# Seven-product SwiGLU in a hybrid decoder trunk: sums and casts behind the evictions, modulation blocks in a load order of their own

## The chip, the core and the metric

One NeuronCore of a Trainium2 chip runs the whole program. The metric is device time in microseconds (us) from launch to end; lower is better. TensorE does the matmuls, VectorE (DVE), ScalarE (ACT) and GpSimd (POOL) the elementwise work, and SyncE (SP) issues nearly all loads. Each engine works its own instructions strictly in the order in which the program wrote them, and waits for the others by semaphores.

## The reference, cut to what matters

Two layers, each: a SwiGLU half step, a mixer (retention, two convolutions), a second SwiGLU half step. Input: 512 prompt tokens and 64 sample tokens, 576 columns in all, model width 1024, inner width 2816, everything in float32.

```python
ada = silu(c) @ w_ada + b_ada            # 9 modulation vectors per sequence and layer
h = rms_norm(x, g) * (1 + scale) + shift
x = x + 0.5 * gate * ((silu(h @ w1) * (h @ w3)) @ w2)
...                                      # mixer, then the same SwiGLU with other weights
```

## The kernel before, in words

**Precision.** A float32 product is made from three matmuls of halves: every operand is split into `hi` (a rounded copy, made by ScalarE) and `lo` (the difference, made by VectorE), and `hi*hi + hi*lo + lo*hi` is summed in PSUM (lines 267 to 269 and 533 to 535). The weights are split in the kernel: `raw` tiles arrive by DMA in four buffers (`RAW`), ScalarE casts `hi` (lines 180 and 194), VectorE subtracts `lo` (line 129, called by `rest`), and five pairs of `hi` and `lo` buffers (`WB`, counted by `live`) hold the results.

**Tiling.** The 576 columns are worked in two halves of 288 (`HB`). One matmul is 128 x 128 weights against 128 x 288 columns. The inner width is 22 blocks `f` of 128 columns of w1 and of w3.

**Seven products.** For f = 4 to 21 two neighbouring blocks of one weight are taken together (a "duo") and the 2 x 2 block product is made with seven block products instead of eight, as Strassen and Winograd do. `duo_step(f, up)` does it for w1 (up = 0) and then for w3 (up = 1) by calling `seven`. In `seven` the seven products run one after another on TensorE, 12 matmuls each, into four PSUM banks: X0 into p, Y0 into q, X1 on top of p, Z0 on top of q, S into r, Y1 into t, Z1 on top of r. ScalarE copies p away between X0 and X1 (line 542, called s1 here), because X1 goes on accumulating on p; VectorE adds s1 and q (line 546, called u here) between Y0 and Z0. Each finished quarter goes to `post`: for up = 0 the silu (`up1`), for up = 1 the product with the silu and the split into `ghi` and `glo` (`up3`; line 835 on POOL, 838 on ACT, 839 on DVE). The sums of weight blocks that the scheme needs are made by POOL: `sums` (lines 204 and 205) when a pair of raw tiles is taken up, and `z` (lines 209 and 210) as a job of its own. The jobs of the next pair (cast X, sums z, casts S, Y, Z) are emitted one by one by `pump`.

**Differences of h.** The scheme also needs sums and differences of h's blocks: `forms` makes them, four rounds of POOL adds (`za`, `zb`, lines 491 and 492), four VectorE operations (495 to 498), ScalarE casts (501 and 502) and VectorE subtractions (504 and 505), a step at a time while the first pairs f = 0 to 3 run as plain products. `last_forms` (lines 517 and 518) then overwrites the second half of four rows of `hh` and `hl` in place, once f = 3 is through.

**Order.** The program is written out by hand: a list of steps (`steps`) is walked once, and `pump` is called at many points. It issues DMAs on SP in the order of one list of keys (raw weights and modulation blocks mixed, in the order of use), emits casts, and emits jobs. In the first SwiGLU of layer 0 and in the second one the modulation matmuls (`ada_unit`, line 332) are sown in between the steps: two units after each duo step and, in the second, after each down step too (one there in the first). After eight units `ada_unit` copies PSUM to SBUF on VectorE (line 337), and `ada_done` transposes the copy on TensorE (line 348) at the next opportunity: at the start of a duo step, of a down step, or in `tick`. `down` does the product with w2: for each of the four groups of f (`GROUPS`) eight down steps, one per block of 128 output columns; a post of them is three VectorE operations (728, 731, 734) and one on POOL.

Below are the functions that the diff touches and what calls them.

Of the kernel before, what the change touches and what calls it, by code (L numbers as in the profile page):

```python
# [69 lines left out]
class Trunk:  # L70
    def __init__(self, nc, tc, d, o, ctx):
# [14 lines left out]
        self.later = []  # L86
        self.quota = 0
# [30 lines left out]
    def start(self):  # L118
# [5 lines left out]
        self.n_dma = self.held = self.whole = self.live = self.cur = 0  # L124
# [6 lines left out]
    def pump(self, later=False):  # L131
        nc = self.nc
        once = False
        while True:
            went = False
            if self.n_dma < len(self.keys) and self.keys[self.n_dma][0] == "do":
# [3 lines left out]
            elif self.n_dma < len(self.keys) and self.keys[self.n_dma][0] == "ada":  # L140
                if self.whole < (ADA if self.quota < 9 else ADA_LATER) and self.n_dma <= self.cur + 2 * ADA:
                    key = self.keys[self.n_dma]
                    self.split[key] = self.slot([128, 512], what="ada")
                    nc.sync.dma_start(self.split[key], self.source(key)[0])
                    self.n_dma += 1
                    self.whole += 1
                    went = True
# [8 lines left out]
            if self.jobs:  # L156
                if not (later and once) and self.live + self.jobs[0][0] <= WB:
# [4 lines left out]
            elif self.raw and self.quota and self.order[self.raw[0][0]] <= self.order[self.cur] + AHEAD:  # L162
# [70 lines left out]
    def free(self, key):  # L233
        if key[0] == "ada":
            self.whole -= 1
# [247 lines left out]
    def forms(self):  # L483
# [4 lines left out]
        zs = []  # L488
        for i in range(4):
            za, zb = self.slot([128, NT], what="za"), self.slot([128, NT], what="zb")  # L490
            nc.gpsimd.tensor_add(za, self.hh[:, i, :NT].bitcast(F32), self.hl[:, i].bitcast(F32))
            nc.gpsimd.tensor_add(zb, self.hh[:, i + 4, :NT].bitcast(F32), self.hl[:, i + 4].bitcast(F32))
            yield
# [15 lines left out]
            zs.append(za)  # L509
# [11 lines left out]
    def seven(self, key, post):  # L521
# [16 lines left out]
        free = lambda which: self.free((*key, which))  # L538
        p, q = bank(), bank()
# [3 lines left out]
        self.rest()  # L543
# [3 lines left out]
        self.rest()  # L547
# [3 lines left out]
        self.rest()  # L551
# [3 lines left out]
        self.rest()  # L555
# [4 lines left out]
        self.rest()  # L560
# [4 lines left out]
        self.rest()  # L565
# [3 lines left out]
        self.rest()  # L569

# [42 lines left out]
    def begin(self, l, sh, pairs, post, forms=()):  # L613
# [26 lines left out]
        for n, pair in enumerate(pairs):  # L640
            hooks = {k: more for k in (1, 3, 5)}
# [103 lines left out]
    def ffn(self, l, ab, sh, fill, first, last):  # L745
# [5 lines left out]
        def post(pair, half, ps):  # L751
            nc = self.nc
            f = pair[0][2]
            if half == 0:
# [28 lines left out]
        def pair_step(pair):  # L783
            ws = [self.use(k) for k in pair]
            for half in range(2):
                ps = []
                for w, k in zip(ws, pair):
                    ps.append(self.run(w, self.h, half))
                    if half == 1:
                        self.free(k)  # L790
                    self.tick()
                post(pair, half, ps)

# [847 lines left out]
```

## Time and profile before

| | |
|---|---|
| median of 3 runs | 3319.72 us (3313.78 to 3321.75) |
| profiled execution | 3321.77 us |
| its span, first to last instruction | 3320.0 us |
| mean granted TensorE clock | 0.964 of full |
| TensorE busy with matmuls | 3072.1 us, 93% of the span |
| VectorE, ScalarE, POOL busy | 1981.4, 1033.6, 1013.0 us |

The profile is of one execution; its own time is 2.05 us above the median. Waits are told as "instruction that waited <- instruction that released it". A matmul's duration in the profile overlaps the next one's, so TensorE's pace is read from counts in a stretch, not from durations. TensorE's clock has two levels here, 2.4 GHz (granted 1.00) and 1.2 GHz (granted 0.50).

### The profile page before, as it was taken

Reading aid. Unit: us, or ns where it says so; the run is one execution under the profiler, and the core shown is the slowest. Engines: PE = TensorE matmul, PEld = TensorE weight load, DVE = VectorE, ACT = ScalarE, POOL = GpSimd, SP = SyncE. Lnnn points to the kernel's source line nnn. Section 1 sums busy time; section 2 is a strip of 40 time slices with the busy share of each in tenths; the row PEclk is TensorE's granted clock in tenths of the full one; section 3 lists DMA queues with packets and bytes.
Section 4 is the critical chain, followed back from the end, with each engine's and each line's share of the span. In section 5 each row is a group of like instructions: output and inputs, shape, how many; then the busy total and the mean of one; then the engine's idle time right before and its main releaser. Section 6 shows DMA issues by size and latency. Waiting matters only on the chain. (4 is left out here: it accounts for less than half of the span.)

```text
span 3320.0 us, 55694 instructions
## 1 busy us (share of the span) xinstructions
PE 3072.1 (93%) x22548; PEld 2928.9 (88%) x22548; DVE 1981.4 (60%) x3545; ACT 1033.6 (31%) x1761; POOL 1013.0 (31%) x985
## 2 busy tenths in 40 slices
PE   7899989999999998798898999999999999989998
PEld 5788888899999997787797989888999999988997
DVE  6454566356995464444567556663569954666566
ACT  4232333222233332222233333332222333333332
POOL 3242344223122031323324334442231220324352
PEclk9999999999999999898998999999999999989999
DMA  6354423335322313534421222233352223122222
GB/s 236 114 177 164 149 74 115 116 90 118 88 77 89 96 61 131 178 131 168 147 90 48 80 89 77 79 119 114 90 118 88 77 89 96 64 65 78 78 87 67
DMA packets 147298, 349.70 MB, mean 105 GB/s; under 512 B 32912, under 2 KB 37264, under 8 KB 147040
## 3 DMA queue, kind: packets, MB, share of 16 engines
q1 hardware_dynamic: 140384, 329.35, 31.2%
q0 software_dynamic: 5504, 15.61, 1.8%
q8 instruction: 177, 2.90, 0.4%
q10 hardware_dynamic: 1152, 1.18, 0.1%
q14 instruction: 81, 0.66, 0.1%
HBM read 328.90 MB, written 12.45 MB: 103 GB/s over the span
## 5 line engine op out<-in xcount | busy, mean ns | idle before, releaser
L129 DVE TENSOR_TENSOR lo<-raw,hi 128x1024 fp32r<-128x1024 f32 (+2 forms) x553 | 704.0, 1278 | 424.1 <-ACT hi L180 330.4
L267 PE MATMUL pl<-hh,hi 128*128 128x288 f32 x2320 | 695.9, 300 | 23.6 <-ACT t L758 23.0
L268 PE MATMUL pl<-hl,hi 128*128 128x288 f32 x2320 | 689.5, 297 | 9.1 <-POOL hl L476 6.4
L269 PE MATMUL pl<-hh,lo 128*128 128x288 f32 x2320 | 688.4, 297 | 1.5 <-DVE lo L129 1.5
L180 ACT CAST hi<-raw 128x1024 fp32r<-128x1024 f32 (+2 forms) x337 | 315.9, 944 | 590.0 <-PE pl L268 316.1
L267 PEld LDWEIGHTS pl<-hh,hi 128*128 128x128 f32 x2320 | 440.2, 190 | 31.3 <-ACT t L758 23.9
L268 PEld LDWEIGHTS pl<-hl,hi 128*128 128x128 f32 x2320 | 440.1, 190 | 12.3 <-POOL hl L476 7.7
L533 PE MATMUL pl<-hh,hi 128*128 128x288 f32 x1152 | 363.2, 315 | 84.7 <-ACT t L542 65.3
L269 PEld LDWEIGHTS pl<-hh,lo 128*128 128x128 f32 x2320 | 439.7, 190 | 1.9 <-DVE lo L129 1.9
L267 PE MATMUL pl<-ghi,hi 128*128 128x288 f32 x1408 | 426.0, 303 | 5.8 <-ACT hi L180 5.8
L269 PE MATMUL pl<-ghi,lo 128*128 128x288 f32 x1408 | 420.7, 299 | 3.4 <-DVE lo L129 3.2
L268 PE MATMUL pl<-glo,hi 128*128 128x288 f32 x1408 | 420.2, 298 | 0.2
L534 PE MATMUL pl<-hl,hi 128*128 128x288 f32 x1152 | 357.5, 310 | 4.6 <-DVE hl L518 4.6
L535 PE MATMUL pl<-hh,lo 128*128 128x288 f32 x1152 | 357.5, 310 | 1.6 <-DVE lo L129 1.6
L533 PEld LDWEIGHTS pl<-hh,hi 128*128 128x128 f32 x1152 | 232.4, 202 | 98.3 <-ACT t L542 69.3
L267 PEld LDWEIGHTS pl<-ghi,hi 128*128 128x128 f32 x1408 | 269.4, 191 | 22.0 <-issue 12.3
L194 ACT CAST hi<-raw 128x1024 fp32r<-128x1024 f32 x216 | 224.4, 1041 | 158.8 <-PE pl L268 89.9
L269 PEld LDWEIGHTS pl<-ghi,lo 128*128 128x128 f32 x1408 | 268.9, 191 | 5.2 <-DVE lo L129 5.2
L268 PEld LDWEIGHTS pl<-glo,hi 128*128 128x128 f32 x1408 | 269.1, 191 | 1.1 <-DVE glo L839 1.1
L737 POOL TENSOR_TENSOR xs<-xs,t 128x64 f32<-128x64 f32 x144 | 65.4, 455 | 648.2 <-DVE t L734 644.8
L534 PEld LDWEIGHTS pl<-hl,hi 128*128 128x128 f32 x1152 | 233.4, 203 | 5.6 <-DVE hl L518 5.6
L535 PEld LDWEIGHTS pl<-hh,lo 128*128 128x128 f32 x1152 | 233.1, 202 | 2.1 <-DVE lo L129 2.1
(247 smaller groups left out, 6133.9 us busy)
## 6 DMA issues: line engine op xcount, KB each, us to landing
ada<-in_ada SPq DMA_DIRECT2D x288, 256.0 KB, 4.1
raw<-in_win SPq DMA_DIRECT2D x120, 512.0 KB, 3.6
raw<-in_w1a SPq DMA_DIRECT2D x44, 512.0 KB, 3.9
raw<-in_w3a SPq DMA_DIRECT2D x44, 512.0 KB, 4.3
raw<-in_w1b SPq DMA_DIRECT2D x44, 512.0 KB, 3.6
raw<-in_w3b SPq DMA_DIRECT2D x44, 512.0 KB, 4.2
raw<-in_w2a SPq DMA_DIRECT2D x48, 384.0 KB, 3.3
raw<-in_w2b SPq DMA_DIRECT2D x48, 384.0 KB, 3.5
```

The lines of the kernel that those rows point to most:

```text
L129: self.nc.vector.tensor_sub(lo, t, hi.bitcast(F32))
L180: nc.scalar.copy(hi[:, :m], t[:, c])
L194: self.nc.scalar.copy(w[0][:, :n], t[:, :n])
L267: mm(ps[:, :HB], hi[:, c], x[0][:, t], start=first, stop=False)
L268: mm(ps[:, :HB], hi[:, c], x[1][:, t], start=False, stop=False)
L269: mm(ps[:, :HB], lo[:, c], x[0][:, t], start=False, stop=last)
L533: mm(ps, hi[:, c], x[0], start=first and i == 0, stop=False, **k)
L534: mm(ps, hi[:, c], x[1], start=False, stop=False, **k)
L535: mm(ps, lo[:, c], x[0], start=False, stop=last and i == 3, **k)
L737: nc.gpsimd.tensor_add(xs, xs, t[:].rearrange("p b t -> p (b t)"))
```

## The change

- `seven`: `part` no longer calls `pump`. After each product's eviction a new `more()` runs the pending `lo` subtractions (`rest`), then whatever lies in `self.after`, then `pump(True)`; after the last product comes `pump(True, False)`, which emits no job but may take up the next pair (`sums`) or a plain cast. So casts and POOL sums now stand behind the eviction that they used to stand in front of. `ada_done` is called inside `seven`, after the third product, and no more at the start of a duo step or of a single down step.
- `up3`: the ScalarE cast of `ghi` is put off together with the subtraction of `glo`, to the next post; the last one of a seven goes into `self.after`, so behind the next seven's s1 (at the end of a group it is done at once).
- `pump`: at most one job per call, and no cast or `sums` after a job in the same call. Once the kernel is under way (`quota > 8`) modulation blocks are taken out of the common list into a queue of their own (`adas`), so raw weights are no longer held up behind them; a used modulation block counts as free only three calls of `pump` later (`gone`).
- `forms`: POOL makes `za` one round ahead, `zb` goes to VectorE, each round is two steps instead of three; `begin` takes two steps per pair (after k = 2 and 5) instead of three.
- f = 3 runs its second half first, and `last_forms` is emitted between the halves.

```diff
+        self.adas, self.gone = deque(), deque()
...
-    def pump(self, later=False):
+    def load_ada(self, key):
+        self.split[key] = self.slot([128, 512], what="ada")
+        self.nc.sync.dma_start(self.split[key], self.source(key)[0])
+        self.whole += 1
+
+    def pump(self, later=False, cast=True):
         nc = self.nc
-        once = False
+        once = not cast
+        self.calls += 1
+        while self.gone and self.gone[0] <= self.calls:
+            self.gone.popleft()
+            self.whole -= 1
         while True:
             went = False
+            if self.quota > 8:
+                while self.n_dma < len(self.keys) and self.keys[self.n_dma][0] == "ada":
+                    self.adas.append(self.n_dma)
+                    self.n_dma += 1
+                if self.adas and self.whole < ADA_LATER and self.adas[0] <= self.cur + 2 * ADA:
+                    self.load_ada(self.keys[self.adas.popleft()])
+                    went = True
...
-                if not (later and once) and self.live + self.jobs[0][0] <= WB:
+                if not once and self.live + self.jobs[0][0] <= WB:
...
-            elif self.raw and self.quota and self.order[self.raw[0][0]] <= self.order[self.cur] + AHEAD:
+            elif self.raw and self.quota and not (once and cast) and self.order[self.raw[0][0]] <= self.order[self.cur] + AHEAD:
...
     def part(self, key, which):
         self.cur = max(self.cur, self.at[key])
-        self.pump(True)
         return self.split[(*key, which)]
...
         if key[0] == "ada":
-            self.whole -= 1
+            if self.quota > 8:
+                self.gone.append(self.calls + 3)
+            else:
+                self.whole -= 1
...
+        whole_a(0)
+        yield
         for i in range(4):
-            za, zb = self.slot([128, NT], what="za"), self.slot([128, NT], what="zb")
-            nc.gpsimd.tensor_add(za, self.hh[:, i, :NT].bitcast(F32), self.hl[:, i].bitcast(F32))
-            nc.gpsimd.tensor_add(zb, self.hh[:, i + 4, :NT].bitcast(F32), self.hl[:, i + 4].bitcast(F32))
-            yield
+            if i < 3:
+                whole_a(i + 1)
+            za, zb = zs[i], self.slot([128, NT], what="zb")
+            nc.vector.tensor_add(zb, self.hh[:, i + 4, :NT].bitcast(F32), self.hl[:, i + 4].bitcast(F32))
...
+        def more():
+            self.rest()
+            for fn in self.after:
+                fn()
+            self.after = []
+            self.pump(True)
+
...
         nc.scalar.copy(s1, p)
-        self.rest()
+        more()
         product(q, "Y", 0, self.T[7], True, True)
...
         post(0, 0, p)
-        self.rest()
+        more()
+        self.ada_done()
...
         post(0, 1, u, r)
         self.rest()
+        self.pump(True, False)
...
-            hooks = {k: more for k in (1, 3, 5)}
+            hooks = {k: more for k in (2, 5)}
...
-            for half in range(2):
+            halves = (1, 0) if pair[0][2] == 3 else (0, 1)
+            for half in halves:
...
+                if half > halves[1]:
+                    self.drain()
+                    self.last_forms()
...
-            self.ada_done()
             if up == 0:
...
-                nc.scalar.copy(hi, s)
-                waiting.append(lambda: nc.vector.tensor_sub(lo, s, hi.bitcast(F32)))
+
+                def halves():
+                    nc.scalar.copy(hi, s)
+                    nc.vector.tensor_sub(lo, s, hi.bitcast(F32))
+
+                waiting.append(halves)
...
-            for fn in waiting:
-                fn()
+            self.after += waiting
+            if f + 2 in [at for at, _ in GROUPS] + [FT]:
+                for fn in self.after:
+                    fn()
+                self.after = []
...
-            self.ada_done()
+            if len(keys) > 1:
+                self.ada_done()
```

## Rows read from the trace of the kernel before

**Rows 1.** The first lines of the profile's page: the span, and busy us, share of the span and count of each engine.
```profile
span 3320.0 us, 55694 instructions
PE 3072.1 (93%) x22548; PEld 2928.9 (88%) x22548; DVE 1981.4 (60%) x3545; ACT 1033.6 (31%) x1761; POOL 1013.0 (31%) x985
```
**Rows 2.** Busy time by stretch: start and end, length, then busy us and count of each engine, granted clock, DMA share and GB/s. The first four are the four SwiGLU stages (the first and second of layer 0, then of layer 1), the last an undisturbed stretch of the mixer.
```profile
60.00:528.00 468.00, 422.21 (x3226) 392.52 (x3224) 258.91 (x421) 145.36 (x243) 157.05 (x134) 0.96 0.41 134
1217.00:1738.00 521.00, 449.76 (x3386) 415.90 (x3384) 263.38 (x435) 147.04 (x250) 160.29 (x138) 0.91 0.40 136
1769.00:2189.00 420.00, 387.06 (x2794) 384.54 (x2792) 260.61 (x409) 145.87 (x250) 161.51 (x138) 0.95 0.26 80
2876.00:3295.00 419.00, 385.58 (x2789) 383.06 (x2789) 258.47 (x406) 143.53 (x247) 161.27 (x138) 0.96 0.23 71
1079.00:1162.00 83.00, 83.00 (x629) 83.00 (x628) 38.72 (x66) 29.05 (x50) 2.79 (x6) 1.00 0.31 96
```
**Rows 3.** The same stretches, TensorE's matmuls into the `pl` banks alone (the 128 x 288 products).
```profile
60.00:528.00 468.00, 393.35 (x2764) 0.96 0.41 134
1217.00:1738.00 521.00, 411.34 (x2792) 0.91 0.40 136
1769.00:2189.00 420.00, 387.06 (x2794) 0.95 0.26 80
2876.00:3295.00 419.00, 385.58 (x2789) 0.96 0.23 71
```
**Rows 4.** Waits of TensorE over the whole run: who waited for whom, us in total, how often, the longest.
```profile
PE pl L533 <- ACT t L542: 65.3, 17, 5.8
PE pm L348 <- DVE t L337: 53.5, 17, 13.1
PE pl L267 <- ACT t L758: 23.0, 4, 8.1
...
PE pl L533 <- ACT hh L517: 14.6, 3, 7.0
...
PE pl L533 <- DVE t L546: 6.7, 5, 1.6
...
PE pl L267 <- ACT hi L180: 5.8, 7, 1.3
PE pl L269 <- DVE lo L129: 4.7, 9, 0.7
PE pl L534 <- DVE hl L518: 4.6, 4, 1.6
```
**Rows 5.** Waits of TensorE in the stage 1769 to 2189 alone, the first line.
```profile
PE pl L533 <- ACT t L542: 20.0, 5, 4.0
```
**Rows 6.** POOL in order of time, in two places of the stage 1769 to 2189: start us, us, instruction, idle time before it and what ended it.
```profile
1793.66 1.28 POOL L209 TENSOR_TENSOR raw<-raw,s 128x512 f32<-128x512 f32 x1 [11.88 <-issue]
...
1796.26 1.41 POOL L491 TENSOR_TENSOR za<-hh,hl 128x576 f32<-128x576 f32 x1
...
1904.43 0.96 POOL L835 TENSOR_TENSOR t<-t,t 128x288 f32<-128x288 f32 x1 [2.16 <-DVE t L834]
...
1906.98 2.28 POOL L204 TENSOR_TENSOR s<-raw 128x512 f32<-128x512 f32 x1
1909.33 1.38 POOL L205 TENSOR_TENSOR raw<-raw,raw 128x512 f32<-128x512 f32 x1
1910.67 1.77 POOL L835 TENSOR_TENSOR t<-t,t 128x288 f32<-128x288 f32 x1
```
**Rows 7.** ACT in order of time, in the same two places, and in a down step of the stage 1217 to 1738 (the first line).
```profile
1344.65 0.83 ACT L180 CAST hi<-raw 128x768 fp32r<-128x768 f32 x1 [10.79 <-DMA raw<-in_w2b]
...
1803.06 0.67 ACT L501 CAST thi<-zb 128x576 fp32r<-128x576 f32 x1 [10.79 <-DVE zb L498]
...
1912.48 0.43 ACT L838 CAST ghi<-t 128x288 fp32r<-128x288 f32 x1 [4.04 <-POOL t L835]
1912.82 1.04 ACT L194 CAST hi<-raw 128x1024 fp32r<-128x1024 f32 x1
1913.76 0.39 ACT L542 COPY t<-pl 128x288 f32<-128x288 f32 x1
```
**Rows 8.** DVE in order of time, in the same two places.
```profile
1797.70 1.63 DVE L495 TENSOR_TENSOR za<-za 128x288 f32<-128x288 f32 x1 [4.17 <-POOL za L491]
...
1903.05 0.68 DVE L129 TENSOR_TENSOR lo<-s,hi 128x512 fp32r<-128x512 f32 x1
...
1904.27 0.45 DVE L839 TENSOR_TENSOR glo<-t,ghi 128x288 fp32r<-128x288 f32 x1
...
1908.39 1.19 DVE L839 TENSOR_TENSOR glo<-t,ghi 128x288 fp32r<-128x288 f32 x1
1909.50 2.30 DVE L129 TENSOR_TENSOR lo<-raw,hi 128x1024 fp32r<-128x1024 f32 x1
...
1913.89 1.23 DVE L129 TENSOR_TENSOR lo<-raw,hi 128x1024 fp32r<-128x1024 f32 x1 [0.49 <-ACT hi L194]
```
**Rows 9.** TensorE's modulation matmuls of one down step of the stage 1217 to 1738, in order of time: two units.
```profile
1337.17 1.07 PE L332 MATMUL pm<-ada,cs 128*32 128x256 f32 x16
```
**Rows 10.** SP's four DMA issues right behind them.
```profile
1337.83 1.75 SPq L144 DMA_DIRECT2D ada<-in_ada  x4
```
**Rows 11.** The page's DMA issues: count, KB each, median us from issue to landing.
```profile
ada<-in_ada SPq DMA_DIRECT2D x288, 256.0 KB, 4.1
```

More of the change, by code (lines that the diff above doesn't have):

```diff
@@ L123, in start @@
         self.raw, self.late, self.split, self.jobs = deque(), deque(), {}, deque()
-        self.n_dma = self.held = self.whole = self.live = self.cur = 0
+        self.n_dma = self.held = self.whole = self.live = self.cur = self.calls = 0
+        self.adas, self.gone = deque(), deque()
     def rest(self):
@@ L140, in pump @@
             elif self.n_dma < len(self.keys) and self.keys[self.n_dma][0] == "ada":
[L141 to L144, printed above, removed]
+                if self.whole < ADA and self.n_dma <= self.cur + 2 * ADA:
+                    self.load_ada(self.keys[self.n_dma])
                     self.n_dma += 1
-                    self.whole += 1
                     went = True
@@ L487, in forms, with whole_a @@
         self.T = {2: [], 4: [], 5: []}
-        zs = []
+        zs = [None] * 4
+        def whole_a(i):
+            zs[i] = self.slot([128, NT], what="za")
+            nc.gpsimd.tensor_add(zs[i], self.hh[:, i, :NT].bitcast(F32), self.hl[:, i].bitcast(F32))
+        whole_a(0)
+        yield
         for i in range(4):
-            za, zb = self.slot([128, NT], what="za"), self.slot([128, NT], what="zb")
-            nc.gpsimd.tensor_add(za, self.hh[:, i, :NT].bitcast(F32), self.hl[:, i].bitcast(F32))
-            nc.gpsimd.tensor_add(zb, self.hh[:, i + 4, :NT].bitcast(F32), self.hl[:, i + 4].bitcast(F32))
-            yield
+            if i < 3:
+                whole_a(i + 1)
+            za, zb = zs[i], self.slot([128, NT], what="zb")
+            nc.vector.tensor_add(zb, self.hh[:, i + 4, :NT].bitcast(F32), self.hl[:, i + 4].bitcast(F32))
             a, b = slice(0, HB), slice(HB, NT)
@@ L508, in forms @@
             self.T[4].append((hi[:, a], lo[:, a]))
-            zs.append(za)
             yield
@@ L550, in seven @@
         post(0, 0, p)
-        self.rest()
+        more()
+        self.ada_done()
         product(q, "Z", 0, self.T[2], False, True)
@@ L554, in seven @@
         nc.vector.tensor_sub(u, u, q)
-        self.rest()
+        more()
         r = bank()
@@ L559, in seven @@
         post(1, 1, v, r)
-        self.rest()
+        more()
         t = bank()
@@ L564, in seven @@
         post(1, 0, v, t)
-        self.rest()
+        more()
         product(r, "Z", 1, quarter(1, 1), False, True)
@@ L753, in post @@
             f = pair[0][2]
-            if half == 0:
+            if f not in g:
                 g[f] = (self.slot([128, NT], F32R, "ghi"), self.slot([128, NT], F32R, "glo"))
@@ L788, in pair_step @@
                     ps.append(self.run(w, self.h, half))
-                    if half == 1:
+                    if half == halves[1]:
                         self.free(k)
@@ L799, in one_pair @@
             pair_step(pairs[f])
-            if f == 3:
-                self.drain()
-                self.last_forms()
         acts = {}
@@ L850, in duo_step @@
             self.seven(pairs[f][up], late if up else up1)
-            for fn in waiting:
-                fn()
+            self.after += waiting
+            if f + 2 in [at for at, _ in GROUPS] + [FT]:
+                for fn in self.after:
+                    fn()
+                self.after = []
             if up and f + 2 == FT:
```

## The prediction, made before the changed kernel was built or run

> **What bounds the kernel now.** I read the page first: TensorE is busy 93% of a span of 3320.0 us [rows 1], so the time is TensorE's work, its idle moments and its slow moments. Which of these can go is read from the stretches. In the mixer 629 matmuls of 128 x 288 fit into 83 us at full clock [rows 2]: 0.132 us each. Each SwiGLU stage does the same number of them [rows 3], and in some the modulation matmuls beside (all of TensorE's count less the `pl` matmuls and the 14 or 18 transposes: 448 in the first stage, 576 in the second [rows 2, 3], at 1.07 us for 16 [rows 9]). What each stage took beyond that work:
>
> - first: 468 - 2764 x 0.132 - 448/16 x 1.07 = 73 us
> - second: 521 - 2792 x 0.132 - 576/16 x 1.07 = 114 us
> - third: 420 - 2794 x 0.132 = 51 us; fourth: 419 - 2789 x 0.132 = 51 us
>
> Together 289 us. Two things make it up. The waits of TensorE inside the products: the eight lines of [rows 4] sum to 178 us. And the clock: 1 minus the granted share, times the length, is 19 + 47 + 21 + 17 = 103 us over the four stages [rows 2]; the level of 1.2 GHz comes where TensorE idles (0.91 in the stage with most idle time, 1.00 in the mixer's stretch with none), so this goes when the waits go. 178 + 103 leaves 8 us unnamed. So every us of wait costs 1.58 us.
>
> **The wait for s1 (65 us).** In the third stage it comes five times, 4.0 us each [rows 5]: where a w3 seven (up = 1) is followed by another seven of the same group (groups of 3, 2 and 3 duos, and one of a single duo, give 2 + 1 + 2). The rows of 1906 to 1914 show the chain. POOL takes the next pair's sums (line 204, 2.28 us; 205, 1.38) before the last product of `post` (835, 1.77, ending at 1912.44) [rows 6]. ACT stands on the cast of `ghi` that needs it, until 1912.48, then casts a weight for 1.04 us, and only then copies s1 away at 1913.76 [rows 7]; X1, which goes on in the same bank, waits. The change takes all three out: the sums come behind `post`, the `ghi` cast behind s1, the weight cast behind s1. In ACT's queue ahead of s1 there remains the cast of the quarter before, whose POOL product is then already done. I count all 65.3 us as removed.
>
> **Transposes waiting for the copy of line 337 (54 us).** Line 337 is queued on DVE behind subtractions that wait for casts that wait for weights; TensorE stands at the transpose because `ada_done` is the first thing of a step. In the change it comes after three products (36 x 0.132 = 4.8 us later), or in a down step after the first half's 16 to 24 matmuls (2.1 to 3.2 us later). The copy itself comes right after the modulation matmuls, so this is enough unless DVE is held up by more. The 13.1 us case is one where it is: ACT and DVE wait for raw tiles. The same cause shows as ACT's 10.79 us for `raw<-in_w2b` [rows 7]: SP issues four modulation loads first [rows 10], each after the matmuls that used its buffer, and the raw key lies behind them in the list. With the queue of their own raw tiles run four ahead. I count 53.5, and the 5.8 and 4.7 us of `ghi` products waiting for weights, as removed.
>
> **forms and last_forms (42 us).** Line 758's silu stands on ACT behind the cast of line 501, which waits for DVE's chain, which waits for `za`, which POOL makes after 209 and 210 [rows 6 to 8]: 23.0 us in four places [rows 4]. With `za` a round ahead and POOL's second add gone, the chain starts a round earlier. On DVE the add of `zb` is 128 x 576; scaled from the 0.68 us of a 128 x 512 subtraction [rows 8] it is an estimated 0.77 us, 16 x 0.77 = 12 us in all, under the plain products that TensorE runs meanwhile (it is 62% busy there [rows 2]); POOL's 1.41 us goes [rows 6]. If that cover failed it would cost those 12 us. The half that `last_forms` overwrites is free 24 x 2 matmuls earlier (6.4 us), so the 14.6 + 4.6 us go too.
>
> Sum removed: 65.3 + 53.5 + 23.0 + 14.6 + 5.8 + 4.7 + 4.6 = 171.5 us of wait, and 58% of it in clock, 99 us: 271 us at most.
>
> **What is given back.** (a) The next thing that is late is u (line 546), which Z0 waits for. In the new order DVE has, before u, the last quarter's operation, the subtraction of the quarter before, the `lo` of Z, and then line 839 of the last quarter, which waits for POOL and ACT. Line 835 and a `lo` subtraction do not run side by side: next to a line 205 of 1.38 us a `lo` took 2.30 us where it takes 1.23 alone, and a line 839 took 1.19 beside line 204 instead of 0.45 [rows 6, 8]; one waits until the other is through. From the end of Z1: 0.45, POOL's 0.96, `lo` 1.23, the sum of line 204 at 1.28 (the undisturbed 209), 839 at 0.45, u at 0.45 make 4.8 us; Z0 would start after 36 x 0.132 = 4.8 us. On top comes what DVE is late at the end of up = 1. That stretch has four POOL sums (4 x 1.28), three POOL products (3 x 0.96), three `lo` at 1.23, one at 0.68 and four 839 at 0.45 to run one after the other: 14.2 us in a seven of 84 x 0.132 = 11.1 us. So up to 3.1 us late; the up = 0 seven has 9.5 us of it and catches up. Bounds: no wait, and the old 4.0 us back. I take 2.0, in the middle, 20 times (5 per stage): 40 us, and a clock share of 30%, between none and the 58%, as short waits lower the clock less often: 52 us.
>
> The Trainium skill (SBUF — State Buffer, section "SBUF: two separate sides") has it that GpSimd and a VectorE operation with two SBUF inputs share a port pair by "an exclusive lock, not a bandwidth split". The rows agree (2.30 us instead of 1.23). By a mere sharing the stretch would have 6 us of DVE work beside 8 of POOL's, and term (a) would be nothing.
>
> (b) Modulation loads in the second stage's down steps. Each uses all four blocks that `ADA_LATER` allows, and a block is reloaded three pump calls later, in the next down step, on SP behind a raw load that waits for ACT's cast (0.83 us [rows 7]) and a subtraction (1.23 x 768/1024 = 0.92 us [rows 8]) after the step's last matmul. With 0.44 us of issue [rows 10] the load leaves 2.2 us after it and lands 4.1 us later [rows 11], at 6.3; the next unit is due at 1.07 + 36 x 0.132 = 5.8 us in groups of six, at 1.07 + 24 x 0.132 = 4.2 in the group of four. Before, SP issued 0.7 to 2.4 us behind the matmuls [rows 9, 10]. With 72 units there are 22 such down steps, 16 of six and 6 of four. Bounds: nothing, and 4.1 us each, 90 us. So it is short by 0.5 and 2.1 us where a raw load stands ahead, in over half of the steps; I take 0.3 x 16 + 1.5 x 6 = 14 us, near the lower bound.
>
> (c) Small remains, one job per pump call among them, which spreads casts: 5 us a stage, 20 us (0 to 40).
>
> Net 271 - 52 - 14 - 20 = 185 us: a span of 3135 us. The profiled execution was 1.8 us longer than its span and 2.05 us above the median, so 3135 us stands against the median of 3319.72.
>
> **Rivals.**
>
> - *All of it comes (3055 us, chance 0.17).* The waits in (a) fall into slack. For: in the first two stages modulation matmuls (1.07 us) lie between sevens. Against: the 14.2 us in 11.1. 3320 - 271 and a few us.
> - *The wait moves from ACT to DVE whole (3210 us, 0.15).* (a) at its upper bound: 20 x 4.0 x 1.58 = 126 instead of 52. For: five waits for line 546 are there already, up to 1.6 us [rows 4].
> - *s1 is not freed (3185 us, 0.07).* The change doesn't do what it says: the `ghi` cast left ahead of s1 waits for a POOL product that stands behind z's sums. 103 us stay, and (a) falls away: 3135 + 103 - 52. Against: z starts some 6 us before that product.
> - *No difference (0.03).* Other work takes each freed place; nothing in the rows names it.
> - *Slower (3500 us, 0.08).* Modulation loads starve TensorE. The place is every step with two units or one, 40 in the first stage and 36 in the second; reload only after three pump calls, behind waiting raw loads. A full reload seen by TensorE is 4.1 + 0.9 us of issue, 76 x 5.0 = 380 us in place of (b). It decides above (185 + 14)/76 = 2.6 us per step. Against: in duo steps the call comes early in an 11 us seven.
> - *The forecast (3135 us, 0.50)*, by itself 3095 to 3175.
>
> Range: 3050 to 3225 leaves out some of the first and second, the no-change and the slower case, about 2 in 10. Faster by over 0.3% 0.89, within 0.3% (about what a measurement can tell here) 0.03, slower 0.08.
>
> **What would show it.** Right: no wait for line 542 in the third stage, none for 348, 758 and 517 of over 1 us; POOL's 204 behind the last 835; granted clock of 0.98 or more in the two stages of layer 1, of about 390 us each; short waits for 546. (b) shows as waits of line 332 for `ada` loads in the second stage. Wrong: waits for 542 that stay, waits for 546 of 3 us and more, or line 332 waiting in duo steps.

## The result, and the profile after

The changed kernel takes 3190.5 us in the median of 4 runs (3188.02 to 3193.01), the kernel before 3317.69 in 4 runs beside them: a ratio of 0.9617, 95% interval 0.960 to 0.963. It is 127 us faster. The forecast was 3135 us, 185 us faster; the range (3050 to 3225) held the time, but 58 us of the gain did not come.

The first lines of the page after, to be read against [rows 1]:

```profile
span 3191.2 us, 55709 instructions
...
PE 3038.2 (95%) x22548; PEld 2881.9 (90%) x22548; DVE 2032.3 (64%) x3561; ACT 1038.3 (33%) x1761; POOL 986.4 (31%) x969
```

The matmuls are the same 22548. POOL has 27 us less work and VectorE 51 more. The sixteen `zb` additions, which changed engines, are 21 of the 51 (1.33 us each, not the estimated 0.77); another 29 are the same 553 `lo` subtractions, which now take 733 us instead of 704. The four SwiGLU stages after (start and end, length, busy us and count of each engine, granted clock, DMA share, GB/s), which answer to the first four lines of [rows 2]:

```profile
60.00:499.00 439.00, 417.60 (x3224) 386.37 (x3223) 272.19 (x425) 146.06 (x243) 147.17 (x130) 0.98 0.43 142
1188.00:1665.00 477.00, 440.44 (x3383) 396.31 (x3382) 276.64 (x438) 147.49 (x250) 154.18 (x134) 0.97 0.44 146
1695.00:2085.00 390.00, 375.08 (x2794) 372.32 (x2792) 272.72 (x413) 147.43 (x250) 155.56 (x134) 0.99 0.27 86
2774.00:3166.00 392.00, 376.96 (x2788) 373.94 (x2788) 270.32 (x410) 145.06 (x246) 155.19 (x134) 0.99 0.24 76
```

They are 29, 44, 30 and 27 us shorter, 130 in all, which is the whole gain (the span fell by 128.8). The waits of TensorE over the whole run, which answer to [rows 4] (line 284 is the old 267, 556 the old 533, 349 the modulation matmul of line 332, 365 the transpose of line 348, 572 the copy of s1, 576 the sum u, 790 the silu of the plain pairs):

```profile
PE pm L349 <- DMA ada<-in_ada: 39.1, 24, 8.0
PE pl L284 <- ACT t L790: 28.8, 11, 5.7
PE pl L556 <- DVE t L576: 20.3, 20, 1.8
...
PE pl L556 <- ACT t L572: 6.6, 4, 2.5
...
PE pm L365 <- DVE t L354: 2.2, 4, 1.2
PE pl L286 <- DVE lo L131: 2.2, 3, 0.7
```

The reader sees two kinds of lines. Gone, as forecast: the wait for s1 (65.3 to 6.6 us), the transposes (53.5 to 2.2), `last_forms` (14.6 + 4.6 to nothing), the weights (5.8 + 4.7 to 2.2 us). Present: waits for modulation blocks (39.1, of which 8.0 is a wait at the start of the program, so 31.1 without it), silu waits that sum to more than before (23.0 in four places, 28.8 in eleven) and twenty waits for u of 1.0 us.

Three stretches show the three. **The modulation blocks**, in the first down step of a group in the second stage. First SP's DMA issues (a line can hold several), then TensorE's modulation matmuls, then one row of ACT and one of VectorE:

```profile
1405.84 3.88 SPq L166 DMA_DIRECT2D raw<-in_w2b  x2
1409.83 0.85 SPq L135 DMA_DIRECT2D ada<-in_ada  x2
1410.73 0.43 SPq L166 DMA_DIRECT2D raw<-in_w1b  x1
1411.25 4.11 SPq L135 DMA_DIRECT2D ada<-in_ada  x4
```
```profile
1404.88 1.07 PE L349 MATMUL pm<-ada,cs 128*32 128x256 f32 x16
1413.27 1.71 PE L349 MATMUL pm<-ada,cs 128*32 128x256 f32 x8 [2.37 <-DMA ada<-in_ada]
1417.98 1.30 PE L349 MATMUL pm<-ada,cs 128*32 128x256 f32 x6 [2.99 <-DMA ada<-in_ada]
```
```profile
1407.21 0.43 ACT L872 CAST ghi<-t 128x288 fp32r<-128x288 f32 x1 [1.78 <-POOL t L867]
```
```profile
1408.41 1.83 DVE L131 TENSOR_TENSOR lo<-raw,hi 128x768 fp32r<-128x768 f32 x2 [0.28 <-ACT hi L195]
```

The matmuls that free the four blocks run from 1404.88 to 1405.95. SP stands on two raw loads, because their buffers are free only after a `lo` subtraction of VectorE. The first leaves at 1405.84, about as the blocks come free. The second leaves at 1409.40: its subtraction is the first of the two at 1408.41, behind a cast that stood on ACT behind the `ghi` cast of the seven's last quarter, which waited for POOL. So the first reload leaves 3.9 us after the modulation matmuls end, and the next unit waits 2.37 us. The unit after it waits 2.99: its blocks are issued from 1411.25, behind another raw load, and the first of them lands 6.7 us later. Waits of this kind at the first down step of the six groups that have modulation units, three in the first stage and three in the second, sum to 24 of the 31.1 us.

**The wait for u**, at the join of two sevens in the third stage, VectorE, POOL and then TensorE:

```profile
1854.15 0.45 DVE L873 TENSOR_TENSOR glo<-t,ghi 128x288 fp32r<-128x288 f32 x1
1854.52 1.82 DVE L131 TENSOR_TENSOR lo<-raw,hi 128x1024 fp32r<-128x1024 f32 x1
1856.26 1.54 DVE L873 TENSOR_TENSOR glo<-t,ghi 128x288 fp32r<-128x288 f32 x1
1857.72 0.44 DVE L576 TENSOR_TENSOR t<-t,pl 128x288 f32<-128x288 f32 x1
```
```profile
1854.31 0.96 POOL L867 TENSOR_TENSOR t<-t,t 128x288 f32<-128x288 f32 x1 [1.89 <-DVE t L864]
1855.22 2.27 POOL L219 TENSOR_TENSOR s<-raw 128x512 f32<-128x512 f32 x1
```
```profile
1858.22 0.40 PE L556 MATMUL pl<-thi,hi 128*128 128x288 f32 x1 [0.83 <-DVE t L576]
```

The POOL sum (219) stands behind the product (867), as the change means it. The subtraction of line 873 takes 1.54 us beside that sum; the same line took 0.45 at 1854.15, before POOL began, and u comes behind it: TensorE waits 0.83 us here.

**The silu wait**, in the plain pairs of the third stage: VectorE, then POOL, ACT and TensorE.

```profile
1721.53 0.75 DVE L528 TENSOR_TENSOR tlo<-zb,thi 128x576 fp32r<-128x576 f32 x1
1722.20 1.55 DVE L529 TENSOR_TENSOR t<-za,t 128x288 fp32r<-128x288 f32 x1
1723.67 1.83 DVE L517 TENSOR_TENSOR zb<-hh,hl 128x576 f32<-128x576 f32 x1
1725.41 1.65 DVE L519 TENSOR_TENSOR za<-za 128x288 f32<-128x288 f32 x1
```
```profile
1721.75 1.68 POOL L224 TENSOR_TENSOR raw<-raw,s 128x512 f32<-128x512 f32 x1 [15.35 <-issue]
1723.51 1.37 POOL L225 TENSOR_TENSOR raw<-raw 128x512 f32<-128x512 f32 x1
1724.84 1.91 POOL L509 TENSOR_TENSOR za<-hh,hl 128x576 f32<-128x576 f32 x1
```
```profile
1728.57 0.67 ACT L525 CAST thi<-zb 128x576 fp32r<-128x576 f32 x1 [8.22 <-DVE zb L522]
...
1729.48 0.40 ACT L790 ACTIVATE t<-pl 128x288 f32<-128x288 f32 x1
```
```profile
1729.94 0.61 PE L284 MATMUL pl<-hh,hi 128*128 128x288 f32 x1 [5.69 <-ACT t L790]
```

The silu is ready to run and stands on ACT behind the cast of line 525, as in the kernel before [rows 7]; that cast waits 8.22 us for VectorE's chain, of which three operations are stretched to 1.55, 1.83 and 1.65 us beside three POOL operations. The last of these is the `za` of the next round, which the change itself moved there. From 1721.53 on the chain takes 7.0 us, for operations that take some 3.8 us undisturbed (an estimate from rows of 0.75 and 0.46 us), so about 3.2 of the 5.69 us come from the stretch.

### The profile page after: what moved, and what is told of

The parts are those of the page before. It is cut to its first block, busy times and chain, and to the rows that moved or that the text cites. A ratio compares the mean times of both kernels' runs of the same rounds, so it can differ in the third digit from the quotient of the medians.

```text
span 3191.2 us, 55709 instructions
## 1 busy us (share of the span) xinstructions
PE 3038.2 (95%) x22548; PEld 2881.9 (90%) x22548; DVE 2032.3 (64%) x3561; ACT 1038.3 (33%) x1761; POOL 986.4 (31%) x969
## 4 chain that ended last, share of the span: by engine, by line
PE 47%; DVE 7%; issue 2%; POOL 2%; DMA 1%; ACT 1%; SPq 0%; DVEq 0%; POOLq 0%; ACTq 0%
PE pl L284 9%; PE pl L285 9%; PE pl L286 9%; PE pl L556 5%; PE pl L558 5%; PE pl L557 5%; DVE lo L131 2%; DMA ada<-in_ada 1%; PE pm L349 1%; DVE glo L873 1%; PE pl L1025 0%; PE pl L1027 0%; PE pl L1026 0%; POOL t L867 0%; PE pm L1424 0%
## 5 line engine op out<-in xcount | busy, mean ns | idle before, releaser
L131 DVE TENSOR_TENSOR lo<-raw,hi 128x1024 fp32r<-128x1024 f32 (+2 forms) x553 | 732.6, 1330 | 241.8 <-ACT hi L195 212.1
L284 PE MATMUL pl<-hh,hi 128*128 128x288 f32 x2320 | 696.4, 300 | 29.1 <-ACT t L790 28.8
L285 PE MATMUL pl<-hl,hi 128*128 128x288 f32 x2320 | 689.2, 297 | 9.1 <-POOL hl L493 6.4
L286 PE MATMUL pl<-hh,lo 128*128 128x288 f32 x2320 | 688.1, 297 | 2.2 <-DVE lo L131 2.2
L284 PEld LDWEIGHTS pl<-hh,hi 128*128 128x128 f32 x2320 | 439.8, 190 | 39.0 <-ACT t L790 32.1
L285 PEld LDWEIGHTS pl<-hl,hi 128*128 128x128 f32 x2320 | 440.0, 190 | 12.3 <-POOL hl L493 7.7
L286 PEld LDWEIGHTS pl<-hh,lo 128*128 128x128 f32 x2320 | 439.7, 190 | 2.9 <-DVE lo L131 2.9
L556 PE MATMUL pl<-hh,hi 128*128 128x288 f32 x1152 | 342.6, 297 | 6.6 <-ACT t L572 6.6
L558 PE MATMUL pl<-hh,lo 128*128 128x288 f32 x1152 | 340.0, 295 | 0.0
L557 PE MATMUL pl<-hl,hi 128*128 128x288 f32 x1152 | 339.6, 295 | 0.0
L556 PEld LDWEIGHTS pl<-hh,hi 128*128 128x128 f32 x1152 | 216.4, 188 | 18.2 <-issue 7.8
L284 PE MATMUL pl<-s,hi 128*128 128x288 f32 x768 | 229.1, 298 | 0.0
L285 PE MATMUL pl<-s,hi 128*128 128x288 f32 x768 | 227.6, 296 | 1.1 <-DVE s L300 1.1
```

What stands on the lines that cost most here:

```text
L131: self.nc.vector.tensor_sub(lo, t, hi.bitcast(F32))
L284: mm(ps[:, :HB], hi[:, c], x[0][:, t], start=first, stop=False)
L285: mm(ps[:, :HB], hi[:, c], x[1][:, t], start=False, stop=False)
L286: mm(ps[:, :HB], lo[:, c], x[0][:, t], start=False, stop=last)
L556: mm(ps, hi[:, c], x[0], start=first and i == 0, stop=False, **k)
L557: mm(ps, hi[:, c], x[1], start=False, stop=False, **k)
```

## The experiments

Each kernel is the changed one with the edit named; times are medians of 4 runs. The kernel before, run beside three groups of them, gave 3319.5, 3316.7 and 3320.9 us. Waits are those of one profiled execution of each.

### Parts of the change undone

**The order inside the seven undone** (`pump` at the first access of a product again and no more behind the evictions, the `ghi` cast at once, nothing carried into the next seven):

```diff
     def part(self, key, which):
         self.cur = max(self.cur, self.at[key])
+        self.pump(True)
...
-                def halves():
-                    nc.scalar.copy(hi, s)
-                    nc.vector.tensor_sub(lo, s, hi.bitcast(F32))
-                waiting.append(halves)
+                nc.scalar.copy(hi, s)
+                waiting.append(lambda: nc.vector.tensor_sub(lo, s, hi.bitcast(F32)))
...
```

> The changed kernel with the order inside the sevens put back: pump before each product, sums, weight casts and the cast of ghi in front of s1 again, nothing carried over into the next seven. All else as changed (modulation queue, forms, half order of f = 3, transposes after the third product, one job per call). Theory 1, that the order inside the sevens frees s1: the waits for the copy of s1 come back to 60 to 70 us and the twenty short waits for u (20.3 us in the changed kernel) go; with a clock share of about 40% that is 3190 + 91 - 24, so 3257 us, 3240 to 3275. Theory 2, that s1 is free because at most one job is emitted per call and the raw tiles come earlier: no more than 15 us of waits for s1, and a time within 10 us of 3190.

Measured: 3219.45 us, 29 more than the changed kernel; neither theory. The waits for s1 came back at 1.2 us each, not 3.8, and those for u did not go:

```profile
PE pl L557 <- DVE t L573: 28.1, 18, 1.6
PE pl L557 <- ACT t L569: 19.6, 17, 2.5
```

The two guards in `pump` could still keep the POOL sums behind the product of the quarter, so they went too.

```diff
-                if not once and self.live + self.jobs[0][0] <= WB:
+                if not (later and once) and self.live + self.jobs[0][0] <= WB:
...
-            elif self.raw and self.quota and not (once and cast) and self.order[...] ...
+            elif self.raw and self.quota and self.order[...] ...
```

> As the run with the seven's order undone (weight work taken on at the first access of each product, the ghi cast straight behind its quarter), and with it the two guards in the weight queue undone: a call that casts may again take on the next pair's POOL sums. Theory 1: the long wait for s1 needs those sums in front of the quarter's POOL product; it comes back whole, 17 x 3.8 = 65 us of wait instead of the 20 of the run without this, and the waits for u go from 28 to under 10: some +30 us of wait and a clock share over that run's 3219, so 3245 to 3275. Theory 2: the sums come behind the product anyway, and the rest of the wait belongs to the transposes at the start of a step: 3210 to 3230, waits for s1 at about 20 us.

Measured: 3273.57 us (ratio to before 0.9864, interval 0.985 to 0.988), 83 us more than the changed kernel. The wait for s1 is more than whole again, 77.7 us in 23 places where it was 65.3 in 17, and the one for u is gone from the list:

```profile
PE pl L557 <- ACT t L569: 77.7, 23, 4.0
```

POOL's rows and ACT's last ones show the chain of [rows 6, 7] again, nearly number for number (line 863 is the POOL product, 867 the `ghi` cast):

```profile
1890.19 2.27 POOL L219 TENSOR_TENSOR s<-raw 128x512 f32<-128x512 f32 x1
1892.54 1.38 POOL L220 TENSOR_TENSOR raw<-raw,raw 128x512 f32<-128x512 f32 x1
1893.88 1.77 POOL L863 TENSOR_TENSOR t<-t,t 128x288 f32<-128x288 f32 x1
```
```profile
1895.68 0.43 ACT L867 CAST ghi<-t 128x288 fp32r<-128x288 f32 x1 [4.04 <-POOL t L863]
1896.02 1.04 ACT L209 CAST hi<-raw 128x1024 fp32r<-128x1024 f32 x1
1896.97 0.39 ACT L569 COPY t<-pl 128x288 f32<-128x288 f32 x1
```

So the order inside the seven with the guards is worth 83 us, and 54 of them came only with the guards, that is with the sums passing the product on POOL. The guards alone were not undone. Theory 1 had the mechanism; the time came out at the upper end of its range.

**The modulation queue undone** (blocks in the common list again, a buffer free at once):

```diff
...
-            if self.quota > 8:
-                self.gone.append(self.calls + 3)
-            else:
-                self.whole -= 1
+            self.whole -= 1
```

> The changed kernel with the modulation blocks back in the common list, a used block free at once. All else as changed. Theory 1, that the queue of their own only moves the wait from weights to modulation blocks: the 39 us of waits of modulation matmuls for loads fall to a few us, waits of products for weights come back with 10 to 15 us, and the time is 3160 to 3190 us. Theory 2, that without it the late raw tiles hold up ACT and DVE and with them much else: waits for weights and transposes of 40 us and more, 3215 us and above.

Measured: 3169.2 us (0.9548, 0.953 to 0.956), 21 us less than the changed kernel. Theory 1: this part of the change costs time. Beyond the start of the program the waits for modulation loads are down from 31.1 to 1.0 us. Those for weights came back with 25 us (10.8 + 4.0 for casts, 6.1 + 4.2 for subtractions), more than the 10 to 15 of the theory, and the transposes' rose from 2.2 to 6.6; those for u fell from 20.3 to 12.3.

**The transposes early in the step again** (`ada_done` at the start of a duo step, and of every down step):

> The changed kernel with the transposes of the modulation copy back at the start of each duo step and each down step. All else as changed. Theory 1, that the copy is late because DVE's queue is always some us behind TensorE: the waits of the transposes come back with 35 us or more, 3235 us or more. Theory 2, that the copy was late because ACT and DVE stood waiting for raw tiles, which now come early: the waits of the transposes stay below 25 us and the time below 3225 us.

Measured: 3223.8 us (0.9714, 0.969 to 0.974), 33 more. The waits at the transposes:

```profile
PE pm L365 <- DVE t L354: 34.3, 17, 5.1
```

32 us of wait for 33 us of time. The theories had 35 us and more for the first and under 25 for the second, and 3235 and 3225 us: the wait is nearly the first's, the time the second's. The waits for modulation blocks are 29.6 us, without the one at the start, as in the changed kernel (31.1). **Both of these undone**:

> The changed kernel with both the place of the transposes and the modulation queue as before. Undone alone, the first cost 34 us and the second gave back 21. Theory 1: the two are independent, and TensorE waits at the transposes as in the run with these alone undone: 3196 to 3210. Theory 2: the queue of their own was what kept raw tiles early, as the prediction had it, and with the transposes early in the step late weights hold them up again (the waits for line 354's copy over 45 us): 3215 to 3240.

Measured: 3215.87 us (0.9679, 0.966 to 0.970), at the lower bound of theory 2, whose sign is in the wait itself:

```profile
PE pm L355 <- DVE t L344: 54.8, 17, 12.5
```

That is nearly the 53.5 us and the 13.1 us of [rows 4] again. So where the transposes are early the queue does take 20 us off their wait (54.8 to 34.3), by earlier raw tiles as the theory has it (the waits for weights are 16 us without it, 2 with it), but it brings 29 us of waits for modulation blocks with it (0.9 to 29.6), and the time is 8 us longer, which is hardly clear of the noise. Where the transposes are late, the queue costs 21 us. The late transposes are what gains: 47 us in the common list (3215.87 to 3169.20), for 48 us of wait. Together the two parts are worth 25 us (47 less 21, unrounded 25.4).

**The change to `forms` undone**:

> The changed kernel with forms as before: za and zb both on POOL in the same step, three steps a round, three steps per pair in begin. Half order of f = 3 and all else as changed. Theory 1, that the change to forms does nothing for the wait for the silu of the plain pairs, which comes from emitting a step of forms ahead of the eviction: that wait stays between 20 and 32 us (28.8 in the changed kernel, 23.0 before), and the time is 3180 to 3200 us. Theory 2, that za ahead and zb on VectorE help as the forecast had it, hidden by something else: the wait grows to 45 us or more and the time to 3210 or more.

Measured: 3195.16 us (0.9624, 0.961 to 0.964), 5 us more by the medians and 2 by the ratios, within the noise, with 28.3 us of silu waits in four places against 28.8 in eleven. Theory 1: moving `zb` to VectorE and `za` a round ahead split the wait and left its sum and the time. **The order of the halves of f = 3 undone** (`last_forms` behind the whole pair):

> The changed kernel with the order of the halves of f = 3 and the place of last_forms as before. Theory 1 (the prediction's step): the 14.6 + 4.6 us for what last_forms writes come back, with a clock share 19 to 30 us: 3209 to 3221. Theory 2: the chain on DVE starts early enough without it: 3187 to 3195.

Measured: 3204.84 us (0.9659, 0.964 to 0.968), 14 more, below theory 1's range: 13.4 us of wait (7.0 for `hh`, 6.4 for `hl`) came back, not 19, and with hardly a clock share: the granted clock of the profiled executions is 0.982 instead of 0.983.

The parts sum: 83 (seven and guards) + 25 (transposes and queue) + 14 (halves) + 5 (forms) = 127 us, the gain itself. By the ratios, each to the kernel before run beside it, the same four sum to 119 of 127, so the closeness is partly luck, but no large part is missing.

### What remains

**The carried half behind u** (the `ghi` cast and the subtraction of line 873 that a seven carries over run one eviction later):

```diff
-        def more():
+        def more(first=False):
             self.rest()
-            for fn in self.after:
-                fn()
-            self.after = []
+            if not first:
+                for fn in self.after:
+                    fn()
+                self.after = []
...
         nc.scalar.copy(s1, p)
-        more()
+        more(True)
```

> The changed kernel, but the ghi cast and the subtraction that a seven carries over into the next one run behind u instead of between s1 and u. Theory 1: u is late because that subtraction (1.54 us at 1856.26 where it takes 0.45 undisturbed) stands ahead of it on DVE: the waits for u fall from 20.3 to under 6 us and the time by 14 to 24 us: 3166 to 3177. Theory 2: u is late by DVE's share against POOL whatever its order, since the lo subtraction ahead of it (1.82 for 1.22) is held as well: u's waits stay above 12 us, 3184 to 3195.

Measured: 3171.27 us (0.9555, 0.954 to 0.957), 19 us less, and 1.0 us of waits for u left. Theory 1. VectorE at the same join (line 874 is the old 873, 577 is u):

```profile
1841.11 0.44 DVE L577 TENSOR_TENSOR t<-t,pl 128x288 f32<-128x288 f32 x1
...
1843.35 1.54 DVE L874 TENSOR_TENSOR glo<-t,ghi 128x288 fp32r<-128x288 f32 x1
```

The subtraction still takes 1.54 us, but behind u, where nobody waits for it. 19.3 us of wait were worth 19 us.

**Reloads ahead of the raw loads** (a block's buffer free after one pump call instead of three, all due reloads at once, and a raw tile's buffer given back five calls later while reloads are due):

```diff
-                self.gone.append(self.calls + 3)
+                self.gone.append(self.calls + 1)
...
-                if self.adas and self.whole < ADA_LATER and ...
+                while self.adas and self.whole < ADA_LATER and ...
...
+    def give(self):
+        if self.adas and self.whole:
+            self.back.append(self.calls + 5)
+        else:
+            self.held -= 1
...
```

> The changed kernel, its modulation blocks in the queue of their own, but reloaded one call after their buffer is free instead of three, all that are due at once, and the raw tile's buffer given back five calls later while reloads are due, so that on SP a reload stands ahead of the raw loads that wait for DVE. Theory 1: the 39.1 us of waits for modulation blocks come from the reload's place behind waiting raw loads: they fall under 18 us (the first load of all, 8, stays), the time by 15 to 30 us, 3160 to 3175. Theory 2: the reload waits for the matmuls that free its buffer, wherever it stands: waits over 30 us, 3185 to 3200, or worse by late raw tiles, 3200 to 3230.

Measured: 3152.39 us (0.9496, 0.948 to 0.951), 38 us less than the changed kernel and the fastest of all. Theory 1's mechanism, with more gain than its range. The waits for modulation blocks, and SP and TensorE at a down step like the one above (line 141 the reload, 175 the raw load, 358 the matmul):

```profile
PE pm L358 <- DMA ada<-in_ada: 14.8, 14, 8.0
```
```profile
1391.30 0.80 SPq L141 DMA_DIRECT2D ada<-in_ada  x2
1392.20 0.38 SPq L175 DMA_DIRECT2D raw<-in_w1b  x1
```
```profile
1390.63 0.64 PE L358 MATMUL pm<-ada,cs 128*32 128x256 f32 x8
1392.17 1.18 PE L358 MATMUL pm<-ada,cs 128*32 128x256 f32 x8 [0.90 <-DMA ada<-in_ada]
1398.47 1.07 PE L358 MATMUL pm<-ada,cs 128*32 128x256 f32 x16
```

Two reloads leave at 1391.30, 0.7 us after the first matmuls began, and the unit at 1398.47 waits for nothing. Without the wait at the start, 31.1 us became 6.8: 24.3 us less of wait for 38 us of time. Which of the three edits did most of it was not tried.

**The eviction first**: in the plain pairs the silu is emitted ahead of the half's background step.

```diff
                     if half == halves[1]:
                         self.free(k)
-                    self.tick()
+                    if len(ps) == 1:
+                        self.tick()
                 post(pair, half, ps)
+                self.tick()
```

> The changed kernel, but in the plain pairs (f = 0 to 3) the eviction with the silu is emitted before the background step of that half instead of behind it, so that the silu is not queued on ACT behind the cast of a form. Theory 1: this place in ACT's queue is the whole cause of the wait for line 790's silu (28.8 us in the changed kernel); it falls under 8 us and the time by 21 to 33 us: 3157 to 3170. Theory 2: DVE's chain under the contention with POOL is what is late, and the stall moves to the forms' own products or to the subtraction behind the silu: 3183 to 3195.

Measured: 3186.95 us (0.9603, 0.959 to 0.962), 3.5 less, within the noise. The silu wait fell to 6.2 us, but the products of the first seven now wait for `last_forms`:

```profile
PE pl L556 <- ACT hh L540: 12.6, 3, 6.1
...
PE pl L284 <- ACT t L790: 6.2, 6, 1.8
```

**And the forms a step earlier** (in `begin` three steps per pair, after k = 1, 3 and 5):

> The run with the eviction emitted first (3187 us), and in the first two pairs of a stage three steps of forms instead of two, so that the chain of forms begins a step earlier in each of the two pairs. Theory 1: the chain of forms simply ends too late in the plain pairs, and each stall that was taken away came back at last_forms (6.07 us in the third and in the fourth stage): both the wait for line 790 (6.2) and that for line 540 (12.6) fall under 4 us, 3166 to 3176. Theory 2: the chain is held by weight work between its steps and not by its beginning: last_forms still waits over 8 us, 3180 to 3190.

Measured: 3185.77 us (0.9597, 0.958 to 0.961): nothing against the run before it. The wait for `last_forms` is gone and the silu's is back:

```profile
PE pl L284 <- ACT t L790: 19.4, 8, 4.8
```

The time is theory 2's, but not by its wait. Two orders of issue moved the stall between two places and left the time; that VectorE's chain of four rounds with its weight work does not fit into the plain pairs is argued from this, and no run with a shorter chain was made.

**Four edits together** (modulation queue undone, carried half behind u, eviction first, forms a step earlier):

> The changed kernel with its modulation queue undone (alone: 21 us faster), the carried half behind u (alone: 19 us), the eviction emitted first in the plain pairs (alone: 3.5) and one more step of forms in each of the first two pairs. Theory 1: the gains are in different waits and add up, with the 15 to 20 us of forms: 3120 to 3140. Theory 2: DVE, which the last two load earlier, takes some of it back at the raw tiles: 3145 to 3160.

Measured: 3158.98 us (0.9513, 0.950 to 0.953), 31.5 less than the changed kernel where the three gains sum to 21 + 19 + 5 = 45. The time is theory 2's, only just, but the wait lists show another reason for most of the missing 13 us. The queue undone had by itself taken 8.0 us of the waits for u (20.3 to 12.3), which the carried half cannot gain again, and a wait of 4.3 us for VectorE's operation of line 846 stands in this run's list alone. The silu still waits 17.4 us.

## Why the prediction was right and wrong

**The sum by parts.** The forecast's 185 us split by its own price of 1.58 us for each us of wait, against what the runs gave:

| part | forecast | measured |
|---|---|---|
| s1, less (a) the waits for u | 103 - 52 = 51 | 83 |
| transposes and weights, less (b) | 101 - 14 = 87 | 25 |
| silu behind the forms' casts | 36 | 5 |
| `last_forms` | 30 | 14 |
| (c) small remains | -20 | not seen apart |

**Right: s1, and what is late next.** The chain was the one told (it stands again in the run with the seven and the guards undone), and u took its place for the reason told: line 873, then u, held beside a POOL sum. The rule of the Trainium skill that was weighed (SBUF — State Buffer, section "SBUF: two separate sides") is in agreement with it, 1.54 us instead of 0.45. The waits for s1 by themselves were worth 83 + 19 = 102 us, against 103 in the sum. Term (a) was 2.7 times too large, 52 us instead of 19: 20 waits of 1.0 us instead of 2.0, and hardly a share of the clock, where the sum had chosen 30%, which no row showed.

**Wrong: term (b).** The step read "with 0.44 us of issue the load leaves 2.2 us after" the step's last matmul, that is a cast of 0.83 us and a subtraction of 0.92 that start at once. In the stretch above it left some 4.9 us after it (1409.83, with the units starting at 1404.88). The raw tile's cast did not start at once: it stood on ACT behind the `ghi` cast of the seven's last quarter, and that one waited for POOL; the same order of rows stands at all six places. The second wait the step did not have at all: blocks issued behind one more raw load took 6.7 us to land, not 4.1. That is why the waits stand mostly at the first down step behind a seven, and why the first stage, which the term left out, has three of these six places. What the working put at 14 us was worth 38 us when most of it was taken away. The slower rival had this mechanism; its place was every step, and it came in the down steps alone.

**Wrong: two cures for one wait.** The sum took the queue of modulation blocks as part of what frees the transposes. The four runs with early and late transposes, with and without the queue, show that the late transposes alone take the wait from 54.8 to 6.6 us, and that the queue brings some 30 us of waits for modulation blocks wherever the transposes stand. The first gained 47 us for 48 us of wait, where the price of 1.58 would have 76; the second gave back 21. The waits for blocks had been 1.4 us in the kernel before and are 1.0 in the changed kernel without the queue.

**Wrong: the forms.** The step read that VectorE's additions lie "under the plain products", because VectorE was 62% busy there. The mean over the stage hid that the chain of `forms` is serial and shares those few us with POOL's sums and the weight work: three operations that take 0.45 and 0.75 us took 1.55, 1.83 and 1.65. The wait that was counted as removed (23.0 us) became 28.8, and with the forms undone it is 28.3. How much of it a chain without the stretch would leave was not tried.

**Wrong: one price for every wait.** The 1.58 came from dividing the whole clock loss by all waits. The runs give different prices: 51 us of wait more (71 for s1, less 20 for u) cost 83 us, and 24.3 us less of modulation waits gave 38, both 1.6; but 19.3 us of waits for u gave 19, 32 us at the transposes cost 33, and 13.4 us at `last_forms` cost 14, all about 1.0. These prices set the waits of one execution against a median of four; by the spans of the profiled executions themselves the five are 1.6, 1.9, 1.1, 1.2 and 0.6, so the first two stay the highest and the sizes are rough. The clock recorded in the traces shows why s1 and u differ: in the kernel before TensorE's clock fell to 1.2 GHz behind 15 of the 17 waits for s1, for 72 us in all; in the changed kernel it fell behind one of the twenty waits for u, for 3.4 us.

The clock's loss was also counted in full although part of it lay within waits, where a slow clock costs nothing. In the four stages the trace of the kernel before has 183 us of waits and 201 us at 1.2 GHz, of which 47 lie inside waits; the trace after has 87, 68 and 12. Time at 1.2 GHz costs half its length, so the waits fell by 96 us and the clock's loss by 67, but (47 - 12)/2 = 18 us of that are the same time counted twice: 145 us for a gain of 130. The other 15 us, found by difference, may be the small remains that term (c) put at 20; no run shows them apart. The granted clock of the span rose from 0.964 to 0.983; with the reloads ahead it is 0.988.

**The signs named ahead.** Right: POOL's sum behind the product; a clock of 0.99 and 390 and 392 us in the stages of layer 1; short waits for 576; waits for modulation loads in the second stage. Wrong: the silu waits of up to 5.7 us, one wait of 1.2 us at a transpose, and in the third stage one wait for s1 of 2.47 us, at its first seven. Of the rivals, "all of it comes" fell to (b), the forms and u; "the wait moves whole" to u's 1.0 us; "s1 is not freed" to the 6.6 us left of it.

## What to carry to other kernels

Where two parts of a change aim at one stall, price each alone and both together: here the later transposes removed the stall, and the load queue meant for the same stall brought a new one. On a queue that issues in order, cost a moved load by every wait ahead of it, not by its own issue, and follow that wait back to its start: here it led over a subtraction and two casts to POOL. And price each wait by itself: by the medians the share that the clock adds differed from nothing to 0.6 us per us, and a mean busy share says nothing about whether a serial chain fits into a short stretch.

## What the runs showed of the hardware that was not expected

- Beside a POOL operation on 128 x 512 or 128 x 576, VectorE's subtractions of 128 x 288 took 1.54 to 1.65 us instead of 0.45, and the addition of 128 x 576 took 1.83 instead of the estimated 0.77 (the subtraction of the same size at 1721.53 took 0.75): the forecast used this for two kinds of rows and left it out for the forms.
- Waits of 1.0 us for u, twenty times, cost no more than their own length, and TensorE's clock fell behind one of them. Waits of 4.0 us for s1 cost 1.6 times theirs, and it fell behind 15 of 17. The transposes' waits with the transposes early again, up to 5.1 us long, lie between: it fell behind 6 of 17, for 27 us in all, and they cost 1.0 by the medians and 1.2 by the profiled executions. Why it fell behind some waits and not behind others of the same length was not settled.
